# A hybrid decoder block on one core: x also loaded transposed, and the first norm's scale moved behind the projections

## The chip, the core and the metric

The kernel runs on one NeuronCore of a Trainium2 chip. Five engines work side by side, each through its own stream of instructions in order: TensorE (PE in the rows; its weight loads are PEld), VectorE (DVE), ScalarE (ACT), GpSimd (POOL) and SyncE (SP, which here only issues DMAs). They wait for one another by semaphores. The metric is the device time of one execution in microseconds (us); lower is better.

## The reference

One layer, 256 tokens, width 1024, float32. The part around the change:

```python
def rms_norm(x, w):
    y = xf * lax.rsqrt(jnp.mean(xf * xf, axis=-1, keepdims=True) + NORM_EPS)
    return (y * w.astype(jnp.float32)).astype(x.dtype)
...
proj = h @ w_in          # h = RMSNorm(x) of the layer, (256, 1024) @ (1024, 3336)
qa, ka, va, qb, kb, vb, qkv_c, z_c, b_c, a_c = jnp.split(proj, split_at, axis=-1)
```

Behind it come two small attentions (A: window of 128 with sinks, B: block-sparse, which at 256 tokens is causal), a gated DeltaNet with a causal convolution of width 4 on its queries, keys and values (`silu(conv(...))`) and a gate `silu(z_c)`, one output projection, a second norm, and a gated feed-forward network (up to 2 x 2816, convolution of width 3, gelu, down).

## The kernel before

Every weight comes from memory as float32 and is cut into two float32r parts, `hi` (a cast on ACT, line 129) and `lo` (the rest, a subtraction on DVE, line 130); so are the activations. A product is three passes: hi by hi, hi by lo, lo by hi. `load` takes a weight block of up to 2048 columns (1 MB) into one of three `raw` buffers (pool `wp`); the next load into that buffer waits on SP until the DVE has read the last of it.

The stages in the order of time:

1. Head (lines 207 to 291). x is loaded row-major as two tiles `xt[0]`, `xt[1]` of 128 tokens. For each tile: sums of squares (`square`, ACT and DVE), `rms_scale` (1/sqrt with one Newton step), the rows times that scale and the weight row `pw` (line 170), eight transposes on PE, then `h_evac` cuts the transposed result into `hT_hi` and `hT_lo` (lines 179, 180). `keep_warm` puts products of ones between. Then the first projection, `pb`: 48 products of 392 columns (line 287) from the weights `wb` (beta, a and the attentions' values).
2. Mixer (the words of `PLAN`). `gdn(c)` for 12 head parts: a projection `pg` (24 products of 256 columns, line 190), the convolution (`cv`: one ACT instruction, line 300, and three on DVE, line 302), a tanh (`th`, line 305), and line 306. `att(c)` for 7 pairs of attention heads: `pa`, brought out by ACT (lines 317, 319). `zgate(n)`: `pz`. Between them stand the small products of the DeltaNet; its inversion (`inv2`) goes round by `p_Y` on PE, `Y` on ACT (line 459), `p_D` on PE, `Dc` on DVE (line 465).
3. The output projection `pm`, the second norm and the feed-forward network (`pu`, `py`).

In the head and around the second norm the order on DVE, ACT and PE is the written one (`manual_schedule`). In the mixer a scheduler sets the order on each engine from its own estimate of durations, so that an edit there can change the order in many places. All DMAs are issued by SP in the written order.

Of the kernel before, what the change touches and what calls it, by code (L numbers as in the profile page):

```python
# [14 lines left out]
P = 128  # L15
# [28 lines left out]
WB0 = 1  # L44
WARM = [3, 2, 0]
# [6 lines left out]
def hybrid_block(ctx: ExitStack, tc, a):  # L52
# [40 lines left out]
    def rms_scale(pool, parts, name, meanwhile=None):  # L93
        """1 / sqrt(mean + eps): the square root's reciprocal, refined by a Newton step."""
# [70 lines left out]
    def norm_transpose(src, r, w, xn, n, name):  # L165
        """rows times r and w, transposed; the caller evacuates"""
# [35 lines left out]
    # =================== token mixer ===================  # L202
    with ExitStack() as mctx:
# [3 lines left out]
        pre = mp.tile([1, D], F32, tag="DL", name="pre")  # L207
        nc.sync.dma_start(pre, a["pre"])
        nc.sync.dma_start(xt[0], a["x"][0:P, :])
        nc.sync.dma_start(cst[:, 0:P], a["cst"][:, 0:P])  # L210
        nc.sync.dma_start(xt[1], a["x"][P:, :])
        nc.sync.dma_start(prm, a["prm"])
        ones = mp.tile([P, P], F32, name="ones")
        G.memset(ones, 1.0)
        def weights(src, c, total, per, store, name):
# [18 lines left out]
        raws = [load(a["wb"][:, c:c + 4].rearrange("p k c -> p (k c)"), f"wb{c}") for c in (0, 4)]  # L234
        nc.sync.dma_start(cst[:, P:], a["cst"][:, P:])
        nc.sync.dma_start(row, a["row"].to_broadcast([P, 12]))
        with tc.manual_schedule(engines={V.engine, A.engine, T.engine}):
            warm(cp, AF.Sqrt, zero, "warm_s")
            pw = []
            for j in range(2):  # L240
                pw.append(mm(f"n1_w{j}"))
                T.matmul(pw[j], ones[0:1, :], pre[0:1, j * 512:(j + 1) * 512], start=True, stop=True)
            xw = [mp.tile([P, D], F32, tag=("R", "gb")[n], name=f"n1_x{n}") for n in range(NT)]
            idle = mm("idle")

            def keep_warm(n):
                """products of ones that nobody reads: the array's clock slows down without work"""
                for i in range(n):
                    T.matmul(hs(idle, i % 4), ones, ones, start=True, stop=True)

            sq1 = [two(kp, "sq", f"n1_sq{n}") for n in range(NT)]

            def square(n):
                for j in range(2):
                    jk, x = kp.tile([P, 512], F32, tag="jk", name=f"n1_j{n}{j}"), xt[n][:, j * 512:(j + 1) * 512]
# [13 lines left out]
            h_evac(p0, 0, 0)
            h_evac(p0, 0, 1)  # L270
            half = 2 * W_BVA
            w = []
            if WB0:
                w = [split(raws[0], 0, half, "wb0", CH_M)]
            h_evac(p1, 1, 0)
            h_evac(p1, 1, 1)
            w += [split(raws[c // 4], c % 4 * W_BVA, half, f"wb{c}", CH_M) for c in (0, 2, 4, 6)[WB0:]]
            keep_warm(WARM[2])
# [31 lines left out]
        def att(c):  # L310
            """two heads' queries (scaled by -1/8 over their slope) or keys"""
# [23 lines left out]
        def gates():  # L335
# [6 lines left out]
            # softplus(y) = max(y, 0) + log1p(e), e = exp(-|y|); log1p(e) = 2 artanh(e / (2 + e))  # L342
# [27 lines left out]
        # decays, masked before the exponential; L = beta k k^T decay below the diagonal  # L370
        # (what L holds on and above the diagonal is never read)
# [15 lines left out]
        def keys():  # L387
            """token-major keys, their norms, L"""
# [190 lines left out]
        def zgate(n):  # L579
# [6 lines left out]
            A.activation(zt, pz, AF.Tanh, scale=0.5)  # L586
# [4 lines left out]
        def outs(n):  # L591
# [12 lines left out]
            f = newton(kp, fv, H, f"f{n}")  # L604
            for h in range(H):
# [121 lines left out]
    # =================== ConvGLU ===================  # L727
# [4 lines left out]
    def up_tokens(i, n):  # L732
        """a gate and up pair, token-major"""
# [166 lines left out]
def _pack(inp):  # L900
# [64 lines left out]
```

## Time and profile before

| what | us |
|---|---|
| median of 3 runs (351.55 to 355.4) | 351.56 |
| span of the profiled execution | 351.1 |
| PE busy in the span | 338.4 (96%) |
| DVE busy in the span | 257.0 (73%) |
| ACT busy in the span | 213.3 (61%) |

The span runs from the first to the last instruction of one profiled execution. The median of the runs is 0.46 us above it; times below are counted from the span's start. A row of the timeline is one instruction, or several alike in a row (x4), with start, length and, in brackets, how long its engine had been idle and what ended that.

### The profile page before, as it was taken

The numbers are of one execution on the slowest core, as the hardware profiler recorded it, in microseconds if no ns is written. First come the engines' busy times: TensorE is split into PE (matmuls) and PEld (weight loads), VectorE is DVE, ScalarE is ACT, GpSimd is POOL, SyncE is SP. The second block draws the span as 40 slices with busy tenths as digits, with TensorE's granted clock in tenths as the row PEclk, the third lists the DMA queues.
The fourth block names the chain that finished last, engine by engine and source line by source line (L and its number), as shares of the span: only waits on it lengthen the run. The fifth ranks groups of instructions, "written<-read, shape, count | busy, mean of one in ns | idle before, by whom it ended". The sixth has DMA issues, their size and how long they took to land.

```text
span 351.1 us, 7200 instructions
## 1 busy us (share of the span) xinstructions
PE 338.4 (96%) x2904; PEld 306.2 (87%) x2904; DVE 257.0 (73%) x531; ACT 213.3 (61%) x455; POOL 10.2 (3%) x26
## 2 busy tenths in 40 slices
PE   7899999999999999999999999999999999999992
PEld 4799898888788986779998999999999999999981
DVE  3969949987516767768879989887686866689443
ACT  4867588654656568755768777555464644655341
POOL 3030110000000000000000000000000000000000
PEclk9999999999999999999999999999999999999999
DMA  7797630073102736563153677772828363330002
GB/s 243 283 342 245 229 119 2 18 257 114 41 3 96 264 119 239 177 244 120 22 220 119 257 296 289 251 261 98 316 101 293 119 241 119 122 119 2 0 29 92
DMA packets 9107, 57.28 MB, mean 163 GB/s; under 512 B 1137, under 2 KB 1393, under 8 KB 2802
## 3 DMA queue, kind: packets, MB, share of 16 engines
q1 hardware_dynamic: 9074, 56.82, 45.2%
q8 instruction: 23, 0.38, 0.4%
q14 instruction: 10, 0.08, 0.1%
HBM read 55.77 MB, written 1.05 MB: 162 GB/s over the span
## 4 chain that ended last, share of the span: by engine, by line
PE 79%; ACT 8%; DVE 7%; DMA 4%; issue 2%; SPq 0%; DVEq 0%; ACTq 0%
PE pu L190 28%; PE py L693 16%; PE pm L693 6%; PE pg L190 4%; PE pa L190 4%; PE pz L198 3%; PE pt L739 3%; DMA wa_raw<-wa 2%; PE pb L287 2%; DVE u L770 2%; DMA xt<-x 2%; PE pv L663 1%; ACT pr L638 1%; PE p_D L463 1%; DVE wd_lo L130 1%
## 5 line engine op out<-in xcount | busy, mean ns | idle before, releaser
L190 PE MATMUL pu<-hT_hi,wu_hi 128*128 128x256 f32 x304 | 84.3, 277 | 0.0
L190 PE MATMUL pu<-hT_lo,wu_hi 128*128 128x256 f32 x304 | 84.1, 277 | 0.0
L190 PE MATMUL pu<-hT_hi,wu_lo 128*128 128x256 f32 x304 | 84.1, 277 | 0.0
L130 DVE TENSOR_TENSOR wu_lo<-wu_raw,wu_hi 128x1024 fp32r<-128x1024 f32 (+1 forms) x54 | 51.6, 984 | 19.2 <-ACT wu_hi L129 19.2
L190 PEld LDWEIGHTS pu<-hT_lo,wu_hi 128*128 128x128 f32 x304 | 57.2, 188 | 0.7
L190 PEld LDWEIGHTS pu<-hT_hi,wu_hi 128*128 128x128 f32 x304 | 57.1, 188 | 0.7
L190 PEld LDWEIGHTS pu<-hT_hi,wu_lo 128*128 128x128 f32 x304 | 57.1, 188 | 0.0
L129 ACT CAST wu_hi<-wu_raw 128x1024 fp32r<-128x1024 f32 (+1 forms) x54 | 44.6, 859 | 16.9 <-PE pu L190 15.3
L770 DVE SCALAR_TENSOR_TENSOR u<-pu,prm,u 128x255 f32<-128x255 f32 (+1 forms) x88 | 41.1, 478 | 5.8 <-ACT u L768 4.6
L693 PE MATMUL py<-wd_hi,mT_hi 128*128 128x512 f32 x88 | 34.4, 391 | 0.1
L693 PE MATMUL py<-wd_hi,mT_lo 128*128 128x512 f32 x88 | 34.5, 392 | 0.0
L693 PE MATMUL py<-wd_lo,mT_hi 128*128 128x512 f32 x88 | 34.3, 394 | 0.0
L130 DVE TENSOR_TENSOR wd_lo<-wd_raw,wd_hi 128x1024 fp32r<-128x1024 f32 (+1 forms) x28 | 27.2, 990 | 2.1 <-ACT wd_hi L129 2.1
L140 ACT CAST mT_hi<-ge 128x256 fp32r<-128x256 f32 x22 | 8.9, 406 | 32.0 <-DVE ge L774 32.0
L190 PE MATMUL pg<-hT_hi,wg_hi 128*128 128x256 f32 x96 | 27.6, 288 | 0.0
L190 PE MATMUL pg<-hT_hi,wg_lo 128*128 128x256 f32 x96 | 27.1, 282 | 0.0
L190 PE MATMUL pg<-hT_lo,wg_hi 128*128 128x256 f32 x96 | 26.9, 280 | 0.1
L768 ACT ACTIVATE u<-pu,prm 128x256 f32<-128x256 f32 x44 | 24.2, 559 | 3.8 <-PE pu L190 3.8
L129 ACT CAST wd_hi<-wd_raw 128x1024 fp32r<-128x1024 f32 (+1 forms) x28 | 22.7, 864 | 4.6 <-DMA wd_raw<-wd 4.6
L693 PEld LDWEIGHTS py<-wd_lo,mT_hi 128*128 128x128 f32 x88 | 16.5, 188 | 3.3
L693 PEld LDWEIGHTS py<-wd_hi,mT_hi 128*128 128x128 f32 x88 | 16.5, 188 | 3.3 <-ACT wd_hi L129 0.3
L693 PEld LDWEIGHTS py<-wd_hi,mT_lo 128*128 128x128 f32 x88 | 16.5, 188 | 3.1
(292 smaller groups left out, 708.3 us busy)
## 6 DMA issues: line engine op xcount, KB each, us to landing
wu_raw<-wu SPq DMA_DIRECT2D x22, 1024.0 KB, 4.9
wd_raw<-wd SPq DMA_DIRECT2D x11, 1024.0 KB, 4.9
wg_raw<-wg SPq DMA_DIRECT2D x6, 1024.0 KB, 5.8
wo_raw<-wo SPq DMA_DIRECT2D x4, 1024.0 KB, 5.0
wa_raw<-wa SPq DMA_DIRECT2D x3, 1024.0 KB, 7.5
wz_raw<-wz SPq DMA_DIRECT2D x2, 1024.0 KB, 5.0
wb_raw<-wb SPq DMA_DIRECT2D x2, 784.0 KB, 7.6
xt<-x SPq DMA_DIRECT2D x2, 512.0 KB, 4.4
```

The lines of the kernel that those rows point to most:

```text
L129: A.copy(hi[:, b:e], raw[:, c + b:c + e])
L130: V.tensor_tensor(lo[:, b:e], raw[:, c + b:c + e], hi[:, b:e].bitcast(F32), ALU.subtract)
L140: return A.copy(hi, src), V.tensor_tensor(lo, src, hi.bitcast(F32), ALU.subtract)
L190: T.matmul(pt[:, :S], x[:, k * P:(k + 1) * P], h[:, k, :], start=(i == 0), stop=(i == 3 * KT - 1))
L198: T.matmul(pt[:, :wd], h[:, k, n * P:(n + 1) * P], x[:, c:c + wd], start=(i == 0), stop=(i == 3 * KT - 1))
L287: T.matmul(pt[n][:, :W_BVA], h[:, k + b, n * P:(n + 1) * P], x[:, b * W_BVA:(b + 1) * W_BVA], start=(s == order[0] and b == 0), stop=(s == ...
L463: T.matmul(pD[sl, s * 32:s * 32 + 32], Y[sl, s, :], Dc[sl, s, :], start=True, stop=True)
L638: A.activation(pr[:, h, o0:o1], pr[:, h, o0:o1], AF.Exp, bias=nm[:, h, n:n + 1], scale=-1.0, accum_out=den[:, h, n:n + 1])
L693: T.matmul(acc[n][j], y[:, ms], x[:, c], start=(first and i == 0), stop=(last and i == 2))
L739: T.matmul(pt[:, :256], h[:, 4 * j + k, n * P:(n + 1) * P], x[:, k * 256:(k + 1) * 256], start=(j + s + k == 0), stop=(j + s + k == 6))
L768: A.activation(t, pu[c][:, :S], AF.Identity, scale=fw[:, c, 2:3], bias=fw[:, c, 3:4])
L770: V.scalar_tensor_tensor(t[:, s:], pu[c][:, :S - s], fw[:, c, 2 - s:3 - s], t[:, s:], ALU.mult, ALU.add)
```

## The change

x is brought in twice: as before in rows, and as `xT` with the 1024 features on the partitions. The host lays `xT` out. `hT_hi` and `hT_lo` are now cut straight from `xT` times the norm's weight (`pre`, now one column per feature, loaded by a DMA on ACT's queue), without the scale of a token; transposes, the row `pw` and `h_evac` fall away in the head. Squares and scale (`rx`) are worked out from the rows later, behind the cuts of `wb`. The scale is applied to products: to `ba` and `va` per token as they are brought out; by `rbc`, a tile that holds the scale along its columns on all partitions (built with a diagonal `dg` and two products `p_r`), to `pg` and `pa` on DVE; by `rh` and in `f` for the gate. `xT` and `wb` come in three pieces each, in turns, ahead of x.

```diff
+WARM = 8
+FIRST = ((0, 2), (2, 4), (4, 8))
+CH_B = W_BVA
...
-        pre = mp.tile([1, D], F32, tag="DL", name="pre")
-        nc.sync.dma_start(pre, a["pre"])
-        nc.sync.dma_start(xt[0], a["x"][0:P, :])
-        nc.sync.dma_start(cst[:, 0:P], a["cst"][:, 0:P])
-        nc.sync.dma_start(xt[1], a["x"][P:, :])
-        nc.sync.dma_start(prm, a["prm"])
+        pre = mp.tile([P, KT], F32, name="pre")
+        nc.scalar.dma_start(pre, a["pre"])
...
+        xT = mp.tile([P, KT, S], F32, tag="gb_xT", name="xT")
+        raws = [wp.tile([P, 2048], F32, tag="raw", name=f"wb{c}_raw") for c in (0, 4)]
+        for k0, k1 in FIRST:
+            nc.sync.dma_start(xT[:, k0:k1, :], a["xT"][:, k0:k1, :])
+            c = k0 % 4 * W_BVA
+            nc.sync.dma_start(raws[k0 // 4][:, c:c + (k1 - k0) * W_BVA], a["wb"][:, k0:k1].rearrange("p k c -> p (k c)"))
+        for n in range(NT):
+            nc.sync.dma_start(xt[n], a["x"][n * P:(n + 1) * P, :])
+        nc.sync.dma_start(cst[:, 0:P], a["cst"][:, 0:P])
+        nc.sync.dma_start(prm, a["prm"])
...
-            square(0)
-            r = rms_scale(kp, sq1[0], "n10", lambda: square(1))
-            keep_warm(WARM[0])
-            p0 = norm_transpose(xt[0], r, pw, xw[0], 0, "n1")
...
+            def h_split(k):
+
+                A.activation(hT_hi[:, k, :], xT[:, k, :], AF.Copy, scale=pre[:, k:k + 1])
+                V.scalar_tensor_tensor(hT_lo[:, k, :], xT[:, k, :], pre[:, k:k + 1], hT_hi[:, k, :].bitcast(F32),
+                                       ALU.mult, ALU.subtract)
+
+            half = 2 * W_BVA
+            w = []
+            for k in range(0, KT, 2):
+                h_split(k)
+                h_split(k + 1)
+                w.append(split(raws[k // 4], k % 4 * W_BVA, half, f"wb{k}", CH_B))
...
+            dg = kp.tile([P, NT, P], F32, tag="jk", name="dg")
+            for n in range(NT):
+                V.tensor_scalar(dg[:, n, :], ident, rx[:, n:n + 1], None, ALU.mult)
+            G.tensor_scalar(rh, rx, 0.5, None, ALU.mult)
...
+            pr = sm("p_r")
+            for n in range(NT):
+                T.matmul(hs(pr, n), ones, dg[:, n, :], start=True, stop=True)
             for n in range(NT):
-                V.tensor_copy(ba[:, n, :], pt[n][:, 384:392])
-                A.copy(va[:, n, :], pt[n][:, :384])
+                V.tensor_scalar(ba[:, n, :], pt[n][:, 384:392], rx[:, n:n + 1], None, ALU.mult)
+                A.activation(va[:, n, :], pt[n][:, :384], AF.Copy, scale=rx[:, n:n + 1])
+            A.copy(rbc, pr[:, :S])
...
+            m = kp.tile([P, S], F32, tag="cm", name=f"cm{c}")
+            V.tensor_tensor(m, pt[:, :S], rbc, ALU.mult)
             t = kp.tile([P, S], F32, tag="cv", name=f"cv{c}")
-            A.activation(t, pt[:, :S], AF.Copy, scale=cw[:, c, 3:4])
+            A.activation(t, m, AF.Copy, scale=cw[:, c, 3:4])
             for s in range(1, 4):
-                V.scalar_tensor_tensor(t[:, s:], pt[:, :S - s], cw[:, c, 3 - s:4 - s], t[:, s:],
+                V.scalar_tensor_tensor(t[:, s:], m[:, :S - s], cw[:, c, 3 - s:4 - s], t[:, s:],
                                        ALU.mult, ALU.add)
...
-                A.activation(aT[:, c, :], pt[:, :S], AF.Copy, scale=qsc[:, i:i + 1])
+                V.scalar_tensor_tensor(aT[:, c, :], pt[:, :S], qsc[:, i:i + 1], rbc, ALU.mult, ALU.mult)
             else:
-                A.copy(aT[:, c, :], pt[:, :S])
+                V.tensor_tensor(aT[:, c, :], pt[:, :S], rbc, ALU.mult)
```

The order on ACT in the head, from the last cuts of `wb` (`wb_hi`) to the first cuts of `wg`, the weights of `gdn`. Before:

```order
L129 CAST wb_hi_201<-wb_raw 128x784
L346 ACT_TABLE_LOAD
L346 ACTIVATE g_ea<-row 128x4
L129 CAST wg_hi_280<-wg_raw 128x1024
L129 CAST wg_hi_284<-wg_raw 128x1024
L129 CAST wg_hi_356<-wg_raw 128x1024
L291 COPY va<-pb_205 128x384
```

And now:

```order
L130 CAST wb_hi_164<-wb_raw 128x392 x2
L273 ACTIVATE n_j_172,sq_129<-xt_67 128x512
L273 ACTIVATE n_j_176,sq_129<-xt_68 128x512
L280 ACTIVATE rs<-rw 128x2
L361 ACT_TABLE_LOAD
L361 ACTIVATE g_ea<-row 128x4
L304 ACTIVATE va<-pb_190,rx 128x384
L304 ACTIVATE va<-pb_191,rx 128x384
L305 COPY rbc<-p_r 128x256
L355 ACTIVATE g_th<-ba 128x8
L130 CAST wg_hi_269<-wg_raw 128x1024
```

Three cuts of `wg` stood ahead of the first `va`; now all of them stand behind squares, scale, `va` and `rbc`.

The order on DVE from the scale of x to the first convolution, with the change; `cm` is the product times `rbc`:

```order
L284 SCALAR_TENSOR_TENSOR rx<-rs,rx 128x2
L287 TENSOR_SCALAR dg<-cst,rx 128x128 x2
L303 TENSOR_SCALAR ba<-pb_190,rx 128x8
L303 TENSOR_SCALAR ba<-pb_191,rx 128x8
L131 TENSOR_TENSOR wg_lo_270<-wg_raw,wg_hi_269 128x1024
L131 TENSOR_TENSOR wg_lo_274<-wg_raw,wg_hi_273 128x1024
L358 SCALAR_TENSOR_TENSOR g_ab<-g_y 128x8
L131 TENSOR_TENSOR wg_lo_350<-wg_raw,wg_hi_349 128x1024
L131 TENSOR_TENSOR wg_lo_354<-wg_raw,wg_hi_353 128x1024
L313 TENSOR_TENSOR cm_302<-pg_277,rbc 128x256
```

Before, the first two `wg_lo` stood ahead of `ba`; now all four stand behind the scale, and the first `cm` behind them.

The order on ACT in the mixer, around the inversion's `Y`. Before:

```order
L300 ACTIVATE cv_1131<-pg_1106,prm 128x256
L459 COPY Y_1174<-p_Y_1141 128x256
L305 ACTIVATE th_1103<-cv_1098 128x256
L129 CAST wz_hi_1525<-wz_raw 128x1024
L305 ACTIVATE th_1136<-cv_1131 128x256
L300 ACTIVATE cv_1248<-pg_1223,prm 128x256
L459 COPY Y_1291<-p_Y_1258 128x256
```

And now:

```order
L474 COPY Y_1183<-p_Y_1150 128x256
L315 ACTIVATE cv_1140<-cm_1138,prm 128x256
L320 ACTIVATE th_1110<-cv_1105 128x256
L320 ACTIVATE th_1145<-cv_1140 128x256
L130 CAST wz_hi_1538<-wz_raw 128x1024
L474 COPY Y_1302<-p_Y_1269 128x256
L315 ACTIVATE cv_1259<-cm_1257,prm 128x256
```

Each `Y` stood behind a `cv`; now it stands ahead of that `cv`.

## Rows read from the trace of the kernel before

**Rows 1.** The page: the span, and busy time of each engine.

```profile
span 351.1 us, 7200 instructions
...
PE 338.4 (96%) x2904; PEld 306.2 (87%) x2904; DVE 257.0 (73%) x531; ACT 213.3 (61%) x455; POOL 10.2 (3%) x26
```

**Rows 2.** Chain that ended last, its longest pieces up to 33 us: start, length, what.

```profile
2.00 5.44 DMA xt<-x
...
14.10 7.47 PE pb L287 x40
21.80 0.86 ACT va L291 x2
22.66 0.96 ACT wg_hi L129
23.66 1.23 DVE wg_lo L130
24.91 7.49 DMA wa_raw<-wa
```

**Rows 3.** Timeline of PE: the first of `pb`, the first of `pg`.

```profile
11.95 1.11 PE L287 MATMUL pb<-wb_hi,hT_hi 128*128 128x392 f32 x4
...
21.76 0.28 PE L190 MATMUL pg<-hT_hi,wg_hi 128*128 128x256 f32 x1
21.88 0.28 PE L190 MATMUL pg<-hT_lo,wg_hi 128*128 128x256 f32 x1
```

**Rows 4.** Groups of ACT by shape, up to 130 us: busy, mean ns of one.

```profile
L305 ACT ACTIVATE th<-cv 128x256 f32<-128x256 f32 x12 | 5.0, 419 | 3.0 <-DVE cv L302 2.7 <-DVE g_g L358 0.2
L129 ACT CAST wb_hi<-wb_raw 128x784 fp32r<-128x784 f32 x4 | 3.2, 856 | 0.0
```

**Rows 5.** Timeline of ACT in the head.

```profile
15.12 1.28 ACT L346 ACT_TABLE_LOAD   x1
...
16.53 1.98 ACT L129 CAST wg_hi<-wg_raw 128x1024 fp32r<-128x1024 f32 x2
```

**Rows 6.** Timeline of DVE in the head: squares, scale, and cuts of `wg`.

```profile
4.46 0.69 DVE L259 CUSTOM_DVE_ANT_0 n_j<-xt 128x512 f32<-128x512 f32 x1 [4.46 <-DMA xt<-x]
...
6.68 1.41 DVE L170 SCALAR_TENSOR_TENSOR n_x<-xt,n_r,n_w 128x512 f32<-128x512 f32 x2
...
17.60 2.36 DVE L130 TENSOR_TENSOR wg_lo<-wg_raw,wg_hi 128x1024 fp32r<-128x1024 f32 x2 [0.30 <-ACT wg_hi L129]
```

**Rows 7.** Stretches (start:end, length, busy time by engine, PEclk, DMA share, GB/s).

```profile
2.00:6.00 4.00, 3.56 (x4) 1.16 (x4) 1.12 (x5) 1.13 (x5) 0.94 (x2) 1.00 0.92 268
6.00:14.00 8.00, 6.98 (x33) 6.03 (x32) 6.85 (x17) 5.45 (x12) 0.99 (x3) 1.00 1.00 396
```

**Rows 8.** One stretch of a microsecond in the head, the same columns for DMA (PEclk, share, GB/s).

```profile
12.00:13.00 1.00, 1.00 1.10 446
```

**Rows 9.** Groups of DVE by shape, up to 130 us: busy, mean ns of one.

```profile
L302 DVE SCALAR_TENSOR_TENSOR cv<-pg,prm,cv 128x255 f32<-128x255 f32 x12 | 5.7, 476 | 0.3 <-ACT cv L300 0.3
...
L306 DVE SCALAR_TENSOR_TENSOR kT<-th,cv 128x256 f32<-128x256 f32 x4 | 1.7, 420 | 0.5 <-ACT th L305 0.5
...
L140 DVE TENSOR_TENSOR mT_lo<-pv,mT_hi 128x256 fp32r<-128x256 f32 x2 | 0.9, 426 | 3.0 <-ACT mT_hi L140 3.0
```

**Rows 10.** Stretches of the mixer (columns as in Rows 7).

```profile
21.80:60.00 38.20, 37.03 (x305) 35.49 (x304) 30.71 (x86) 28.06 (x77) 6.43 (x12) 1.00 0.51 174
60.00:75.00 15.00, 14.91 (x349) 13.11 (x349) 14.34 (x37) 9.91 (x30) 0.19 (x1) 1.00 0.29 89
```

**Rows 11.** Chain that ended last in the mixer, around two of the inversion's steps.

```profile
77.41 0.47 ACT cv L300
77.88 0.27 ACT Y L459
...
83.48 0.36 ACT cv L300
```

**Rows 12.** PE's last product, and its granted clock behind it (stretches).

```profile
344.22 0.40 PE L693 MATMUL py<-wd_lo,mT_hi 128*128 128x512 f32 x1
...
349.40:349.60 0.20, 0.00 (x0) 0.57 0.97 369
```

More of the change, by code (lines that the diff above doesn't have):

```diff
@@ L43 @@
 BORD = "00 01 02 10 11 12 20 21 22 30 31 32"
-WB0 = 1
-WARM = [3, 2, 0]
+WARM = 8
+FIRST = ((0, 2), (2, 4), (4, 8))
+CH_B = W_BVA
 WO = "40 41 50 51 60 00 10 20 30 70 u u 610 710 010 110 210 310 | 611 711 011 111 | 211 311"
@@ L233, in hybrid_block @@
         wz, wg, wa = [], [], []
-        raws = [load(a["wb"][:, c:c + 4].rearrange("p k c -> p (k c)"), f"wb{c}") for c in (0, 4)]
         nc.sync.dma_start(cst[:, P:], a["cst"][:, P:])
         nc.sync.dma_start(row, a["row"].to_broadcast([P, 12]))
+        rw = mp.tile([P, NT], F32, name="rw")
+        rx = mp.tile([P, NT], F32, name="rx")
+        rh = mp.tile([P, NT], F32, name="rh")
+        rbc = mp.tile([P, S], F32, name="rbc")
         with tc.manual_schedule(engines={V.engine, A.engine, T.engine}):
@@ L238, in hybrid_block @@
             warm(cp, AF.Sqrt, zero, "warm_s")
[L239 to L243, printed above, removed]
-            idle = mm("idle")
-            def keep_warm(n):
-                for i in range(n):
-                    T.matmul(hs(idle, i % 4), ones, ones, start=True, stop=True)
@@ L251, in hybrid_block @@
-            sq1 = [two(kp, "sq", f"n1_sq{n}") for n in range(NT)]
-            def square(n):
+            idle = mm("idle")
+            for i in range(WARM):
+                T.matmul(hs(idle, i % 4), ones, ones, start=True, stop=True)
+            sq1 = mp.tile([P, 2, NT], F32, name="sq1")
+            def h_split(k):
+                A.activation(hT_hi[:, k, :], xT[:, k, :], AF.Copy, scale=pre[:, k:k + 1])
+                V.scalar_tensor_tensor(hT_lo[:, k, :], xT[:, k, :], pre[:, k:k + 1], hT_hi[:, k, :].bitcast(F32),
+                                       ALU.mult, ALU.subtract)
@@ L254, in square @@
+            half = 2 * W_BVA
[5 more added lines that the diff above has]
+            for n in range(NT):
                 for j in range(2):
                     jk, x = kp.tile([P, 512], F32, tag="jk", name=f"n1_j{n}{j}"), xt[n][:, j * 512:(j + 1) * 512]
-                    if n or j:
-                        A.activation(jk, x, AF.Square, accum_out=sq1[n][j])
+                    if j:
+                        A.activation(jk, x, AF.Square, accum_out=sq1[:, j, n:n + 1])
@@ L258, in square @@
                     else:
                         V.tensor_tensor_reduce(out=jk, in0=x, in1=x, scale=1.0, scalar=0.0, op0=ALU.mult, op1=ALU.add,
-                                               accum_out=sq1[n][j])
-            square(0)
-            r = rms_scale(kp, sq1[0], "n10", lambda: square(1))
-            keep_warm(WARM[0])
-            p0 = norm_transpose(xt[0], r, pw, xw[0], 0, "n1")
-            keep_warm(WARM[1])
-            r = rms_scale(kp, sq1[1], "n11")
-            p1 = norm_transpose(xt[1], r, pw, xw[1], 1, "n1")
@@ L269, in hybrid_block @@
[L269 to L278, printed above, removed]
+                                               accum_out=sq1[:, j, n:n + 1])
+            V.tensor_scalar(rw, sq1[:, 0], -0.5 / D, -0.5 * EPS, ALU.mult, ALU.add)
@@ new lines, in hybrid_block @@
+            V.scalar_tensor_tensor(rw, sq1[:, 1], -0.5 / D, rw, ALU.mult, ALU.add)
+            rs = kp.tile([P, NT], F32, name="rs")
+            A.activation(rs, rw, AF.Sqrt, scale=-2.0)
+            V.reciprocal(rx, rs)
+            V.tensor_tensor(rs, rx, rx, ALU.mult)
+            V.tensor_tensor(rs, rs, rw, ALU.mult)
+            V.scalar_tensor_tensor(rx, rs, 1.5, rx, ALU.add, ALU.mult)
+            dg = kp.tile([P, NT, P], F32, tag="jk", name="dg")
+            for n in range(NT):
+                V.tensor_scalar(dg[:, n, :], ident, rx[:, n:n + 1], None, ALU.mult)
@@ L284, in hybrid_block @@
                 x, h = passes(*w[k // 2], hT_hi, hT_lo)[i]
-                for n in range(NT):
-                    for b in range(2):
+                for b in range(2):
+                    for n in range(NT):
                         T.matmul(pt[n][:, :W_BVA], h[:, k + b, n * P:(n + 1) * P], x[:, b * W_BVA:(b + 1) * W_BVA],
                                  start=(s == order[0] and b == 0), stop=(s == order[-1] and b == 1))
+            pr = sm("p_r")
             for n in range(NT):
-                V.tensor_copy(ba[:, n, :], pt[n][:, 384:392])
-                A.copy(va[:, n, :], pt[n][:, :384])
+                T.matmul(hs(pr, n), ones, dg[:, n, :], start=True, stop=True)
+            for n in range(NT):
+                V.tensor_scalar(ba[:, n, :], pt[n][:, 384:392], rx[:, n:n + 1], None, ALU.mult)
+                A.activation(va[:, n, :], pt[n][:, :384], AF.Copy, scale=rx[:, n:n + 1])
+            A.copy(rbc, pr[:, :S])
         def gdn(c):
@@ L585, in zgate @@
             zt = kp.tile([P, 512], F32, tag="jk", name=f"zt{n}")
-            A.activation(zt, pz, AF.Tanh, scale=0.5)
+            A.activation(zt, pz, AF.Tanh, scale=rh[:, n:n + 1])
             V.scalar_tensor_tensor(zg[:, n].rearrange("p h c -> p (h c)"), zt, 1.0, pz, ALU.add, ALU.mult)
@@ L604, in outs @@
             f = newton(kp, fv, H, f"f{n}")
+            V.tensor_scalar(f, f, rx[:, n:n + 1], None, ALU.mult)
             for h in range(H):
@@ L936, in _pack @@
     o["row"] = np.concatenate([g["swa_sinks"], g["dn_a_log"], g["dn_dt_bias"]], 1)
-    o["pre"] = g["mix_pre_norm"]
+    o["pre"] = np.ascontiguousarray(pp(g["mix_pre_norm"][0]))
     o["post"] = np.ascontiguousarray(np.stack([g["mix_post_norm"][0], g["ffn_pre_norm"][0]])[None])
@@ L940, in _pack @@
     o["x"] = np.ascontiguousarray(g["x"][0])
+    o["xT"] = np.ascontiguousarray(g["x"][0].reshape(S, KT, P).transpose(2, 1, 0))
     i, j = np.meshgrid(ar(P), ar(P), indexing="ij")
```

## The prediction

> **What bounds the kernel now.** I read the page first: PE is busy in 96% of a span of 351.1 us [rows 1], so a change pays only if PE's row of work starts sooner or has fewer holes. Then the chain that ended last, which shows where the start is set: x's second tile comes in for 5.44 us, norm and transposes follow, and from 14.10 on 40 products of `pb` run for 7.47 us, 0.187 us each [rows 2]. The timeline of PE gives the head's frame: `pb` begins at 11.95, the first `pg` at 21.76, and products of `pg` follow at 0.12 us, 24 to a head, 2.83 us [rows 3]. The 48 of `pb` need 9.0 us, so some 12.8 us of the first 21.76 hold nothing that counts. From 21.8 to 60 PE is idle 38.2 - 37.03 = 1.2 us, from 60 to 75 only 0.1 [rows 10]: behind the head PE runs nearly without holes, and what the head saves reaches the end of the run if the feeding of PE keeps up. The last thing to see is that the feeding is tight as well: the chain goes from `va` over a cut of `wg` to a DMA of 7.49 us [rows 2], because a raw buffer is loaded again only when DVE has read it, and DVE is busy 14.34 of 15 us from 60 to 75 [rows 10].
>
> **The change: the head.** Everything ahead of `pb` on PE goes: the products of `pw`, 16 transposes, their wait. What sets `pb` now is memory. The rows give 268 GB/s for the first 4 us of traffic and 396 after that [rows 7]. `xT` and `wb` together are 1.05 + 1.61 = 2.65 MB; with 1.07 MB by 6 us the rest takes 1.58/0.396 = 4.0 us, to 10.0, and x's two tiles were used 0.5 and 1.3 us after their last byte by the same count (at 4.46 [rows 6] and 7.44 [rows 2]); with 0.9, the last piece of `wb` is there at L = 10.9. Its earlier pieces are cut while later ones arrive. Behind L, ACT casts two pieces of 392 columns, two of `hT_hi` and two more of `wb`. A cast of 784 takes 0.86 and one instruction of 256 columns 0.42 [rows 4], so 0.43 and 0.37 at back-to-back pace, 2.5 us in all; DVE ends its last cut at L + 3.2. PE needs 24 products, 4.5 us, from L + 0.5 on, so `pb` ends at L + 5 = 15.9, some 5.9 us sooner than before.
>
> But `pg` can't follow. ACT and DVE take in order: squares, 0.61 each on DVE, to L + 4.4; then the scale. From the start of the square to the scaled rows took 6.68 - 4.46 = 2.2 us with one square in it [rows 6], so 1.6 for the scale, to L + 6.0; `dg`, two small instructions, to L + 6.5; `p_r` on PE to L + 7.0. On ACT a table load of 1.28 [rows 5] runs beside that, then come `g_ea`, `va` (0.86 [rows 2]), `rbc` (0.37), `g_th`: L + 7.9. Only now is `wg` cut: `wg_hi` 1.0 us (1.98 for two [rows 5]), `wg_lo` 1.18 (2.36 for two [rows 6]). Four products of `pg` need `hi` alone, the fifth waits for `wg_lo`, at L + 10.1. From there PE runs on, with 4 x 0.12 us done: as if it had begun at L + 9.6 = 20.5. Before it was 21.76. **The head gains 1.2 us.** Cover: `wg`'s own first load stands behind 5.44 MB now, 1.05 more than before; 6 + (5.44 - 1.07)/0.396 + 0.9 = 17.9, against 18.8 (L + 7.9) at which ACT wants it. So two chains end within a microsecond of each other, and taking one away would give little. With 396 GB/s from 2 us on L would be 1.3 us earlier; with 268 up to 10 us, 1.3 later: the head gains between 2.5 and -0.1 us.
>
> The Trainium skill ("DMA: Bandwidth & Descriptors", section "Bandwidth") holds that loads from memory are bound by about 358 GB/s per core, not by the 435 of the fabric. The rows here show 446 in a microsecond of the head [rows 8], so it is not taken; with 358 from 6 us on, L would be an estimated 0.4 us later and the head's gain 0.8.
>
> **The change: DVE and ACT in the mixer.** Each of 12 heads gets a `cm` on DVE: 256 columns from a product and a second operand, 0.43 as the nearest row has it, while its three `cv` now read a copy in SBUF: 0.42 instead of 0.476 each [rows 9]. Net 12 x (0.43 - 0.16) = 3.2 us. Seven `aT` move from ACT to DVE, 0.43 each: 3.0 us. DVE has 6.2 us more work in the mixer, ACT 3 us less. Bounds for PE: nothing, if all of it falls into DVE's holes, or 6.2 us. Up to 60 us DVE has 38.2 - 30.71 = 7.5 us of holes and about half of the new work; from 60 to 75 it has 0.66 [rows 10] and gets four `cm` less 12 savings, 1.1 us. I take 0.7 us: the second stretch's overhang of 0.4 and a little for waits at `cm`, with DVE standing still until `pg` is done.
>
> Against it stands a thing the order shows: each `Y` of the inversion now precedes the `cv` that it stood behind. On the chain those two `cv` are worth 0.47 and 0.36 us [rows 11]: -0.8. ACT is strictly in order, so this holds unless the new `cv`, which waits for `cm`, holds up a later `Y`; then it is 0. A raw buffer of `wg` comes free some 2 us later than before, but its load then has 5.7 us of PE's work on the other pair as cover. The new factor in `f` (two instructions on 128x4) I take at nothing: PE has `pa` products meanwhile; uncovered it is 0.3 us. The feed-forward part is untouched.
>
> **Sum:** -1.2 - 0.8 + 0.7 = -1.3 us. The span of 351.1 becomes 349.8; the median lies 0.46 above that execution's span, so 351.56 - 1.3 = 350.3 us. By the bounds (head -2.5 to +0.1, inversion -0.8 to 0, DVE 0 to 1.8, above which it is the first rival) it is 348.3 to 353.5.
>
> **Rivals.** *DVE becomes the bound* (ends slower). Place: 33 to 90 us, where `cm` sits in front of everything that uses a product. If the whole 6.2 us falls on PE: 351.56 - 1.2 + 6.2 = 356.6; half of it gives 353.5. It decides when DVE's holes between 60 and 75, 0.66 us, don't take what is added there and PE stands waiting for a `lo`. For it: 14.34 of 15; against it: products are released by one `cm` instead of four readers, and the holes ahead of 60.
>
> *Memory is faster than the rows of the ramp.* The slow start [rows 7] may come from the small pieces of `cst` and `prm`, which now stand behind x. With 446 GB/s throughout [rows 8] from 1.6 us on, L = 8.5, `wg` lands at 14.7, and PE is as if it began at 18.1: -3.7, with the inversion -0.8 and nothing for DVE: 347.1 us. Not more, as the row of squares, scale, `va` and cuts stays. For it: no small piece is ahead of `wb`. Against it: pieces are smaller than x's rows were.
>
> *The clock of PE falls.* Between the end of `pb` and `wg_lo`, 15.9 to 21.0, PE has only `p_r` and four products. Behind the last product of the run, at 344.62, the granted clock was half, 1.2 instead of 2.4 GHz, from about 349.4 on [rows 12]; all of the head ran at 1.00 [rows 7]. If it falls here, 24 to 48 products of `pg` take 0.24 instead of 0.12 us: +2.8 to +5.7, so about 353.1 to 356. The hole is 5 us long but not empty. The Trainium skill ("TensorE: Matmul & The Clock Gate", section "HAM oscillation — how this bites in real kernels") says that waits for DMA between bursts of products put the clock down and make the next burst start slow; here, by it, the sum would be the same 353.1, and the trace of before, whose head had holes too, does not show it.
>
> **How the numbers follow.** Forecast 350.3 (348.3 to 353.5): 0.55. Faster memory, 347.1: 0.17. DVE as the bound, 353.5 to 356.6: 0.17. Clock: 0.08. Something else: 0.03. The range takes in the second case and the lower half of the third and fourth: 346.6 to 354.4. Two per cent, 7.0 us, is about what a measurement of this kernel can tell from no change. A gain beyond 344.5 would need the whole 5.9 us of `pb` and more: 0.02. A loss beyond 358.6 needs all of DVE's work and a slow clock on PE's path: 0.04. Within: 0.94.
>
> **What would show it.** `pb` starting near 6 and ending near 16 us; a hole on PE from there to about 20 to 21, ended by DVE's `wg_lo` and not by a DMA; the first continuous `pg` a microsecond before 21.76. In the mixer `Y` without a `cv` ahead of it, and no new waits of PE on DVE over half a microsecond. It is wrong if `wg_hi` waits for its DMA for over a microsecond, if the granted clock leaves 1.00 before 30 us, or if DVE has no hole from 33 to 75 and PE gets one.

## The result, and the profile after

The changed kernel takes 354.67 us (median of 20 runs, 353.29 to 359.02) against 351.75 for the kernel before beside it (20 runs, 351.3 to 355.7). The ratio is 1.0061, 95% interval 1.0035 to 1.0086: slower by about 0.6%, where 1.3 us less was forecast, and 0.3 us outside the stated range. The ratios in this text are taken from the fast runs alone and are no quotients of the medians (here 1.008); two runs of the changed kernel, 358.94 and 359.02 us, are slow ones. The profiled execution took 355.75, a microsecond over the median, with a span of 354.0 us.

The page of the changed kernel, the lines that answer to [rows 1]: the span is 2.9 us more while PE's busy time is 1.2 less, although the head's old work on PE is gone: some of what is left must have become longer, and there are 4.1 us more of holes.

```profile
span 354.0 us, 7204 instructions
...
PE 337.2 (95%) x2894; PEld 307.6 (87%) x2894; DVE 262.4 (74%) x556; ACT 214.8 (61%) x454; POOL 10.3 (3%) x27
```

PE's timeline in the changed kernel (start, length, line, operation, in brackets the idle time ahead of it and who ended it), the lines that answer to [rows 3]. `pb` begins at 6.33 and ends at 17.1 (said: near 6 and 15.9). Then comes the hole, with `p_r` alone in it. The first `pg` starts at 21.22, half a microsecond sooner than before; but products follow each other at 0.21 us until 27.6, and at 0.12, the pace before, only from there.

```profile
6.33 1.68 PE L297 MATMUL pb<-wb_hi,hT_hi 128*128 128x392 f32 x4 [1.53 <-ACT wb_hi L130]
7.80 1.51 PE L297 MATMUL pb<-wb_hi,hT_lo 128*128 128x392 f32 x4
...
16.20 0.88 PE L297 MATMUL pb<-wb_lo,hT_hi 128*128 128x392 f32 x4
18.41 0.77 PE L301 MATMUL p_r<-dg,ones 128*128 128x128 f32 x4 [1.33 <-DVE dg L287]
21.22 0.58 PE L191 MATMUL pg<-hT_hi,wg_hi 128*128 128x256 f32 x1 [2.04 <-ACT wg_hi L130]
...
22.76 0.41 PE L191 MATMUL pg<-hT_hi,wg_lo 128*128 128x256 f32 x1
22.97 0.41 PE L191 MATMUL pg<-hT_hi,wg_hi 128*128 128x256 f32 x1
...
29.71 0.28 PE L191 MATMUL pg<-hT_hi,wg_hi 128*128 128x256 f32 x1
29.82 0.28 PE L191 MATMUL pg<-hT_lo,wg_hi 128*128 128x256 f32 x1
```

Stretches of a microsecond of the same kernel; the third number from the end is the granted clock of PE. It falls at about 20.8, after a stretch in which PE has next to nothing, to 0.50 (1.2 of 2.4 GHz), and is back at about 27.6. In the kernel before this column is 1.00 up to 349 us.

```profile
19.00:20.00 1.00, 0.18 (x2) 0.00 (x0) 0.00 (x0) 1.00 (x3) 0.19 (x1) 1.00 1.07 442
20.00:21.00 1.00, 0.00 (x0) 0.00 (x0) 0.00 (x0) 1.00 (x3) 0.39 (x2) 0.88 0.98 410
21.00:22.00 1.00, 0.78 (x2) 0.50 (x2) 0.80 (x1) 1.00 (x3) 0.00 (x0) 0.50 0.85 352
...
27.00:28.00 1.00, 1.00 (x8) 1.00 (x7) 0.31 (x1) 0.00 (x0) 0.00 (x0) 0.71 0.99 393
28.00:29.00 1.00, 1.00 (x11) 1.00 (x10) 1.00 (x3) 0.85 (x2) 0.69 (x1) 1.00 1.01 410
```

Every run is on record with the mean of its granted clock. It is 0.981 to 0.993 in the 20 runs of the changed kernel, and 0.994 to 0.998 in 79 of the 80 runs of the kernel before that stand beside the experiments (0.990 in one). So the other runs of the changed kernel had more of the low clock too. The mean takes in every fall, that behind the last product as well, so it does not say where a run's clock fell.

What the hole waits for is seen on ACT and DVE of the same kernel (answers to [rows 5, 6]). The last piece of `wb` is there at 11.81, and from it the row goes over casts, squares, `rs`, table load, `va` and `rbc` to the cut of `wg` at 20.11; DVE is done with the first `wg_lo` at 22.4.

```profile
11.81 0.94 ACT L130 CAST wb_hi<-wb_raw 128x392 fp32r<-128x392 f32 x2 [1.04 <-DMA wb_raw<-wb]
...
17.24 1.28 ACT L361 ACT_TABLE_LOAD   x1
...
18.80 1.05 ACT L304 ACTIVATE va<-pb,rx 128x384 f32<-128x384 f32 x2
19.75 0.37 ACT L305 COPY rbc<-p_r 128x256 f32<-128x256 f32 x1
...
20.11 3.90 ACT L130 CAST wg_hi<-wg_raw 128x1024 fp32r<-128x1024 f32 x4
```

```profile
21.20 2.36 DVE L131 TENSOR_TENSOR wg_lo<-wg_raw,wg_hi 128x1024 fp32r<-128x1024 f32 x2 [2.29 <-ACT wg_hi L130]
```

Groups of DVE by shape up to 130 us in the changed kernel (busy, mean ns of one), which answer to [rows 9]: the `cv` cost as much from SBUF as they did from the product's bank, so `cm` comes on top in full, 5.0 us.

```profile
L317 DVE SCALAR_TENSOR_TENSOR cv<-cm,prm,cv 128x255 f32<-128x255 f32 x12 | 5.7, 475 | 0.3 <-ACT cv L315 0.3
...
L313 DVE TENSOR_TENSOR cm<-pg,rbc 128x256 f32<-128x256 f32 x12 | 5.0, 418 | 2.4 <-PE pg L191 2.3
```

Where the time came from, by the first product of each kind on PE in the two profiled executions (before, after): `pg` 21.8, 21.2; `pa` 33.1, 35.5; `p_D` of the inversion 64.5, 66.0; `pz` 87.9, 90.8; `pt` 160.0, 162.6; last `py` 344.2, 346.8. So 2.4 us are lost between `pg` and the first `pa`, and about as much is still missing at the end. In most runs here the time lies 1.8 us above the execution's span; by that (an estimate) the profile of the kernel before, with its 351.1, shows an execution some 1.3 us longer than the median one, and its marks are late by up to as much. In the inversion there is one thing more, PE's waits from 60 to 92 us (in all, how often, the longest): two stops inside `p_D` for which the trace names nothing that PE waited for (0.7 in one stop in the kernel before).

```profile
PE p_D L478 <- issue: 2.1, 2, 1.1
PE p_D L478 <- ACT Y L474: 0.7, 1, 0.7
```

### The profile page after: what moved, and what is told of

It reads as the page before. It is cut to its first block, busy times and chain, and to the rows that moved or that the text cites. A ratio compares the mean times of both kernels' runs of the same rounds, so it can differ in the third digit from the quotient of the medians.

```text
span 354.0 us, 7204 instructions
## 1 busy us (share of the span) xinstructions
PE 337.2 (95%) x2894; PEld 307.6 (87%) x2894; DVE 262.4 (74%) x556; ACT 214.8 (61%) x454; POOL 10.3 (3%) x27
## 4 chain that ended last, share of the span: by engine, by line
PE 77%; DVE 10%; ACT 7%; DMA 2%; issue 1%; SPq 1%; DVEq 0%; POOL 0%; ACTq 0%
PE pu L191 28%; PE py L709 16%; PE pg L191 6%; PE pm L709 6%; PE pa L191 3%; PE pt L755 3%; PE pz L199 3%; DMA wb_raw<-wb 2%; DVE u L786 2%; PE pv L679 1%; DVE cv L317 1%; DVE wg_lo L131 1%; PE p_D L478 1%; ACT wg_hi L130 1%; DVE wd_lo L131 1%
## 5 line engine op out<-in xcount | busy, mean ns | idle before, releaser
L191 PE MATMUL pg<-hT_hi,wg_hi 128*128 128x256 f32 x96 | 29.0, 303 | 2.2 <-ACT wg_hi L130 2.2
L191 PE MATMUL pg<-hT_lo,wg_hi 128*128 128x256 f32 x96 | 28.0, 292 | 0.0
L191 PEld LDWEIGHTS pg<-hT_hi,wg_hi 128*128 128x128 f32 x96 | 19.3, 201 | 3.2 <-ACT wg_hi L130 2.7
L709 PEld LDWEIGHTS py<-wd_hi,mT_hi 128*128 128x128 f32 x88 | 16.5, 188 | 3.5 <-ACT wd_hi L130 0.5
L709 PEld LDWEIGHTS py<-wd_lo,mT_hi 128*128 128x128 f32 x88 | 16.5, 188 | 3.3
```

Source lines behind the costliest of these rows:

```text
L191: T.matmul(pt[:, :S], x[:, k * P:(k + 1) * P], h[:, k, :], start=(i == 0), stop=(i == 3 * KT - 1))
L709: T.matmul(acc[n][j], y[:, ms], x[:, c], start=(first and i == 0), stop=(last and i == 2))
```

## The experiments

Theory A: the hole lets PE's clock fall, and `pg` at half speed is the loss. Theory B: DVE's added work in the mixer is the loss. Two more came up on the way, C (the order that the scheduler gives the mixer) and D (idle products help by something other than filling the hole). "The kernel before" is the one run beside each group, 351.84 to 352.07.

**Idle products in the hole.**

```diff
+            for i in range(6):
+                T.matmul(hs(idle, i % 4), ones, ones, start=True, stop=True)
             pr = sm("p_r")
             for n in range(NT):
                 T.matmul(hs(pr, n), ones, dg[:, n, :], start=True, stop=True)
+            for i in range(11):
+                T.matmul(hs(idle, i % 4), ones, ones, start=True, stop=True)
```

> The changed kernel with 17 idle products of `ones` in the hole of PE's row: 6 between `pb` and `p_r`, 11 between `p_r` and `pg`. They compute nothing that is used. Theory A (PE's clock falls because of the hole between the end of `pb`, 17.0, and the start of `pg`, 21.2, and that is the loss): the granted clock stays at 1.00 from 20 to 28 us, the first `pa` product starts at about 33.0 instead of 35.5, and the time comes to 351.3 to 352.3, 2.4 to 3.4 under the changed kernel. Theory B (the added work of DVE in the mixer, 12 `cm` and 7 `aT`, is the loss): the first `pa` may come earlier, but the gain is gone by the end of the mixer, and the time stays at 353.8 to 354.9.

Measured: 351.48 us, ratio 0.9982 (0.9957 to 1.0007). In the profiled execution the clock is 1.00 from 12 to 340 us (in the head, ahead of the hole, it is 0.50 from 7.6 to 11.0), `pg` starts at 20.7 and the first `pa` at 32.2. The time is 3.2 us under the changed kernel by the medians, 2.8 by the ratios, as theory A has it. Theory B is out as the main cause, since DVE's work is all there. But the order of the mixer is another one here, which leaves theory C.

**The cut of `wg` ahead of `va`, without and with idle products.**

```diff
             G.tensor_scalar(rh, rx, 0.5, None, ALU.mult)
+            weights(a["wg"], 0, N_GDN, 2, wg, "wg0")
```

> The changed kernel with the first cut of `wg` ahead of `va`, `rbc` and `ba` in the rows of ACT and DVE; nothing is added. Theory A: the cut starts when ACT has loaded its table, about 17.3 to 18.5, instead of at 20.1, so `pg` can start at 18.5 to 19.5, the hole is half as long, and either the clock does not fall (then pg starts 2 us sooner at full clock, first `pa` at 31.5 to 32, time 349.5 to 350.5) or it falls for a shorter stretch (352 to 353.5). Theory B: `pg` starts sooner, but the `cm` and `cv` of DVE and ACT wait for `rbc` and run later; the time is 353.5 to 355.

> Both edits: the cut of `wg` ahead of `va`, and idle products in what is left of the hole (6 ahead of `p_r`, 4 behind it). Theory A: the clock stays at 1.00, `pg` starts at about 19.5, the first `pa` at about 31.3; time 349 to 350.5, 4 to 5.5 under the changed kernel and 1 to 2.5 under the kernel before. Theory B: no lower than 353.

Measured: 353.66 (352.08 to 355.05) without, ratio 1.0046 (1.0016 to 1.0076); 349.36 with 6 and 4 idle products, ratio 0.9938 (0.9921 to 0.9954), and 350.37 when it was run again, twelve times (0.9949, 0.9911 to 0.9988).

> The kernel with the first cut of `wg` ahead of `va` and 10 idle products, once more in more rounds, as a version to keep: Theory A gives what it gave, 349 to 350.5, a ratio to the kernel before of 0.992 to 0.997.

Without idle products `pg` starts at 19.1, two microseconds sooner, and in the profiled run (352.25) the clock holds from 11.1 us to the end of the work; still the time is 352 to 355, above what theory A gave for that case; the median is what theory B said. But the same edit with the hole filled, and with all of DVE's work, is 3 to 4 us faster, as theory A had it and theory B excluded. So an earlier start alone is not what pays, though by the traces the mixer's order differs between these two as well. Whether the clock fell behind the hole in the runs that took 354 is not shown: only one was profiled, and the mean clock (0.986 to 0.990 in the four runs from 353.66 on, 0.993, 0.993 and 0.988 in the three below 352.5) takes in the falls in the head and behind the last product.

**The scale left out.** The first kernel, with `m = pt` in `gdn` and `aT` copied by ACT.

> The first of these kernels (17 idle products in the hole) with the scale of the tokens left out behind `pg` and `pa`: `cv` reads the product's bank and `aT` is copied by ACT, as in the kernel before, so the 12 `cm` and 7 `aT` leave DVE (about 8 us of its work). What is left out is the factor of the norm on those rows. Theory A: the added work lies beside PE's, so this comes to within 0.7 of the kernel with the scale, at 351 to 352. Theory B: it is 2 or more faster than that one.

Measured: 352.99, ratio 1.0037 (1.0019 to 1.0055): 1.5 us *slower* than with the scale. Neither theory had that. PE's waits from 30 to 60 us in this kernel name a new one, for the gates' `DL` on ACT; in the kernel with the scale none of them is over half a microsecond.

```profile
PE p_G L425 <- ACT DL L397: 2.1, 2, 1.1
```

The instructions of the mixer stand in another order here, because the scheduler plans with what there is; so a kernel with less work for DVE is not simply a faster one. That made theory C a question of its own.

**The hole filled by 9 and by 10.** One row of the first edit, with 9 ahead of `p_r` and none behind it, then with 10. The run with 9 was meant to fill the hole and leave the order as it is in the changed kernel.

> The changed kernel with 9 idle products between `pb` and `p_r` and none behind `p_r`. Every other instruction stands in the order of the changed kernel, on each engine (in the first of these runs, with 17, the scheduler also put the mixer's `cm`, `cv` and cuts in another order). The products fill 17.0 to 19.2, and the hole that is left is 19.6 to 21.2. Theory A (the clock alone): the clock stays at 1.00, the first `pa` comes at 32.3 to 32.8 in place of 35.5, all later marks are 2.4 to 3.2 earlier, and the time is 351.6 to 352.4. Theory C (the gain of the kernel with 17 came from its order): the time stays at 353.8 to 354.9. Theory B (DVE's added work): the same, 353.8 to 354.9.

> One idle product more, 10. With it the scheduler gives the mixer the order of the kernel with 17 idle products. Theory A: the clock stays as in the run with 9, and what differs from it is the order's part: 0 to 1.0 faster, 351.2 to 352.2. Theory C: 2 to 3 faster than the run with 9, at 351 to 352, while that stays above 353.8.

Measured: 351.57 with 9, ratio 1.0002 (0.9976 to 1.0029); 351.90 with 10, 0.9990 (0.9949 to 1.0031). The whole gain is there with both. But the order did not stay. By the traces the kernels with 9, 10 and 17 idle products run every engine's instructions in one and the same order, and it is not that of the changed kernel. ACT shows it, first in the changed kernel, then in that with 9: a cut of `wa` stands ahead of the first `cv` in the one, and both cuts stand behind it in the other.

```profile
24.45 1.04 ACT L130 CAST wa_hi<-wa_raw 128x1024 fp32r<-128x1024 f32 x1 [0.34 <-DMA wa_raw<-wa]
...
28.15 0.51 ACT L315 ACTIVATE cv<-cm,prm 128x256 f32<-128x256 f32 x1 [2.65 <-DVE cm L313]
```

```profile
25.48 0.51 ACT L317 ACTIVATE cv<-cm,prm 128x256 f32<-128x256 f32 x1 [1.71 <-DVE cm L315]
25.90 1.98 ACT L130 CAST wa_hi<-wa_raw 128x1024 fp32r<-128x1024 f32 x2
```

So what the two texts above say of the order with 9 is not what ran: all three kernels with the hole filled have the other order, and they do not tell theory A from theory C. Within one order the clock can still be seen. Of the ten runs with 9, the five with a mean granted clock of 0.997 or 0.998 have a median of 351.12 us, the five with 0.992 or 0.993 one of 352.49. With 10 it is 351.86 (0.997 and 0.998) against 352.68 (0.989 and 0.990). With 17 no such difference is to be seen: 0.989 goes with 351.44 to 351.78, 0.994 to 0.996 with 351.12 to 351.93.

PE's timeline and two stretches of the kernel with 9 (each idle product and each `p_r` stands as two instructions): PE is at work to 19.4, the hole that is left is 1.5 us, and in this execution the clock stays. The first `pa` comes at 33.1, where 32.3 to 32.8 was expected.

```profile
16.75 2.17 PE L300 MATMUL idle<-ones 128*128 128x128 f32 x18
18.75 0.61 PE L303 MATMUL p_r<-dg,ones 128*128 128x128 f32 x4
20.87 0.38 PE L191 MATMUL pg<-hT_hi,wg_hi 128*128 128x256 f32 x1 [1.50 <-ACT wg_hi L130]
```

```profile
20.00:21.00 1.00, 0.13 (x1) 0.13 (x2) 0.15 (x1) 1.00 (x2) 0.35 (x2) 1.00 0.98 410
...
22.00:23.00 1.00, 1.00 (x9) 0.99 (x9) 1.00 (x2) 1.00 (x2) 0.00 (x0) 1.00 0.32 115
```

**Nine at the start, and four in the hole.** In the first `WARM = 8` becomes 17; the second has `range(4)` where the kernel above has 9. By their traces both do keep the order of the changed kernel.

> A control for the run with 9 idle products in the hole: the changed kernel with 9 more idle products at the start instead (17 in place of 8, ahead of `pb`, from about 3.8 to 6.0), none in the hole. The order of all other instructions is that of the changed kernel. Theory A: the hole between `pb` and `pg` is as before, the clock falls in it as it did, and the time stays at 354 to 355.2. If idle products help by anything else than filling the hole (theory D: they keep PE warm in the first microseconds, or move PE's row), it comes down to 351.5 to 352.5 as with 9 in the hole.

> 4 idle products in place of 9 ahead of `p_r`, in the same order of instructions. They end at about 18.0, before `p_r` at 18.4 to 19.0, so PE's last work ahead of the hole ends at the same time as in the changed kernel, and only the first part of the hole is filled. Theory A as it stands (an almost empty stretch is what lets the clock fall) does not say where the line lies: if the clock holds, 351.3 to 352.3; if it falls later or for a shorter time, 352.5 to 354.5. A time between, with runs of both kinds, would say that the hole is then near the line.

Measured: 355.22 with nine at the start, ratio 1.0053 (1.0015 to 1.0091), the changed kernel's time. So nine products ahead of `pb` do not help, and theory D falls in that form; that nine in the hole help by the order that goes with them is theory C. With four in the hole 353.90 (351.98 at best), ratio 1.0019 (0.9980 to 1.0059), between the two. Stretches, first of the kernel with nine at the start, then of that with four in the hole: in the first the clock falls at 20.7, in the second only at 22.1, and stays low for 3.4 us.

```profile
20.00:21.00 1.00, 0.51 (x2) 0.30 (x2) 0.77 (x1) 1.00 (x2) 0.00 (x0) 0.84 1.00 418
```

```profile
21.00:22.00 1.00, 0.61 (x4) 0.60 (x5) 1.00 (x2) 1.00 (x2) 0.00 (x0) 1.00 0.67 279
22.00:23.00 1.00, 1.00 (x7) 1.00 (x6) 1.00 (x3) 1.00 (x2) 0.06 (x1) 0.57 0.12 33
...
25.00:26.00 1.00, 1.00 (x8) 1.00 (x8) 0.13 (x1) 0.00 (x0) 0.23 (x1) 0.72 0.99 401
```

Note the stretch from 22 to 23: PE is fully at work when the clock falls there. The fall comes behind the hole, not in it. One of the ten runs with four has a mean clock of 0.996, as high as the kernel before, and takes 351.98; the other nine have 0.986 to 0.993, and none of them takes less than 353.14. This kernel has the order of the changed one, so here the loss goes with the clock while the order stays. But it is one run, and it was not profiled.

**The mixer's half alone.** The kernel before with `rbc` as a tile of ones and the `cm` and `aT` of the changed kernel.

> The kernel before with the mixer's half of the change alone: `rbc` is a tile of ones, and the 12 `cm` and 7 `aT` are on DVE as in the changed kernel; its head is as it was, and the result is the same. Theory A: DVE's extra work (some 6 us) lies beside PE's, so the time stays within 0.7 of the kernel before: 351.1 to 352.5. Theory B: it is slower by 2 or more, 353.8 or later. Theory C would show as up to 1.5 either way, since the scheduler gives this kernel an order of its own.

Measured: 353.32, ratio 1.0048 (1.0007 to 1.0089): 1.5 us slower than the kernel before, between what the two theories said. PE has no new wait on `cm` over half a microsecond; its longest in the mixer is 1.2 us for `Y`. So the added work, with the order that goes with it, is not free. But its price and that of the kernel without the scale (1.2 us over the kernel before, with the new head) don't add up to the changed kernel with its hole filled, which stands at 0.0: each of these kernels has an order of its own, and no run here shows what an order is worth by itself.

**The hole filled with PE's own next work.** The first load of `wg` goes ahead of x's rows, its cuts and 48 products ahead of the scale.

```diff
+        wg0 = load(a["wg"][:, 0:2].rearrange("p t c -> p (t c)"), "wg0")
         for n in range(NT):
             nc.sync.dma_start(xt[n], a["x"][n * P:(n + 1) * P, :])
...
+            for c in range(2):
+                wg.append(split(wg0, c * 1024, 1024, f"wg{c}", CH_M))
...
+            pg = [mm(f"pg{c}") for c in range(2)]
+            for c in range(2):
+                proj_cm(pg[c], wg[c])
             pr = sm("p_r")
```

> The changed kernel, with the first load of `wg` ahead of the loads of x in rows, and its two cuts and the first 48 products of `pg` ahead of the squares, `p_r`, `va` and `rbc`: no idle products, but the hole is filled with PE's own next work. Theory A: `pg` starts at 17.5 to 18.5, right behind `pb`; the clock stays at 1.00; the first `pa` comes at 29 to 30.5 and the time is 347 to 349, if the scale that comes later (`rbc` at 23 to 24.5) does not hold `cm` up; with that, 349 to 351. Theory B: no better than 352, since DVE's work is the same and begins later.

Measured: 356.74, ratio 1.0123 (1.0056 to 1.0190), the slowest of all (4 runs, 347 to 351 expected). `pg` does start at 16.2. But the hole has moved. PE's timeline: behind `p_r` it has two products until the third and fourth heads' weights are cut, at 25.0, and these cuts stand on ACT behind `va` and `rbc`, on DVE behind `cm`.

```profile
21.63 0.61 PE L307 MATMUL p_r<-dg,ones 128*128 128x128 f32 x4
23.75 0.39 PE L191 MATMUL pg<-hT_hi,wg_hi 128*128 128x256 f32 x1 [1.50 <-ACT wg_hi L130]
...
25.00 0.39 PE L191 MATMUL pg<-hT_hi,wg_lo 128*128 128x256 f32 x1 [0.76 <-DVE wg_lo L131]
```

```profile
24.00:26.00 2.00, 1.24 (x8) 1.04 (x8) 2.00 (x4) 2.00 (x4) 0.00 (x0) 0.86 0.26 102
26.00:28.00 2.00, 2.00 (x11) 2.00 (x11) 2.00 (x5) 2.00 (x5) 0.00 (x0) 0.50 0.00 0
```

The clock falls again, and once more at 83.5 us, behind a stop of 3.1 us in `p_D` of the unnamed kind:

```profile
82.01 0.28 PE L485 MATMUL p_D<-Dc,Y 32*32 32x32 f32 x9 [3.06 <-issue]
```

The moved hole is not what makes this kernel the slowest. Its first `p_D` comes at 63.0, level with the kernels with 9 and 17 idle products (63.1 and 62.6); from there to the first `pz` it takes 26.8 us, against 21.7 and 22.5. The loss lies in the inversion, where the stop and the second fall are. So my expectation of the time was wrong, but this run does not show that own work is worse than idle products.

**A version to keep.** The kernel with the cut of `wg` ahead of `va` and 6 and 4 idle products, and `wg`'s first load ahead of the rest of the constants on SP:

```diff
-        nc.sync.dma_start(cst[:, P:], a["cst"][:, P:])
-        nc.sync.dma_start(row, a["row"].to_broadcast([P, 12]))
...
             weights(a["wg"], 0, N_GDN, 2, wg, "wg0")
+            nc.sync.dma_start(cst[:, P:], a["cst"][:, P:])
+            nc.sync.dma_start(row, a["row"].to_broadcast([P, 12]))
```

> The same with the first load of `wg` ahead of the loads of the rest of the constants (482 KB, some 1.2 us at 400 GB/s) and of `row` on SP; ACT's table load then stands behind the first cut, since its `g_ea` waits for `row`. Theory A: `pg` starts at 18.0 to 19.0 in place of 19.4, the clock stays, and the time is 348.3 to 349.5, unless the mixer's order, which the scheduler makes anew, takes 0.5 to 1 back.

Measured: 349.85 (349.38 to 352.38, 12 runs), ratio 0.9918 (0.9884 to 0.9952). It beats both kernels, the one before by 0.8% and the changed one by some 1.4%. It is a little over the 348.3 to 349.5 expected, and the intervals do not tell it from the kernel without this last edit (0.9911 to 0.9988). The cut of `wg` begins at 16.42, ahead of the table load, and in the profiled execution the clock holds from 11 us on; `pg` starts at 19.2, since the idle products now end later than the cut asks for.

## Why the prediction was wrong

**The step that failed** is the clock of PE, which the sum put at nothing: it took the products of `pg` behind the hole at 0.12 us, and left the clock to the third rival at a chance of 0.08. In the profiled execution the clock is at 0.50 from 20.8 to 27.6, and 23 products at 0.213 in place of 0.118 us make 2.2 us on PE's row, which from 22.8 on has no hole in which to hide them. The rival had the place and the mechanism right. Its price, 2.8 to 5.7, was too high, and that the time lies in its 353.1 to 356 is in part luck, as the -1.3 of the rest was not there either (below).

How much of the loss is the clock's is shown less well. With the hole filled the time is 351.57, and with the same nine products put elsewhere it is 355.22; between the changed kernel and the filled hole lie 3.1 us by the medians, 2.1 by the ratios. The products account for 2.2 of that. But filling the hole also gave the mixer another order, so these runs by themselves don't part the clock from the order. For the clock speak the lengths of the products, the first `pa` behind them, 2.4 us later than in the kernel with 9, and the one run of 351.98 in the changed kernel's order.

Two arguments held the chance down. "The hole is not empty": `p_r` and four products didn't keep the clock up. "All of the head ran at 1.00 [rows 7]": the column said so, but it was no evidence. In the changed kernel four products of `pb` take 1.51 us at 7.80 and 0.88 at 16.20, and in the kernel before PE's timeline has eight equal transposes at 1.91 and at 1.44 us (these begin behind a wait), all with the column at 1.00:

```profile
7.55 1.91 PE L173 MATMUL n_p<-cst,n_x 128*128 128x128 f32 x8
...
10.76 1.44 PE L173 MATMUL n_p<-cst,n_x 128*128 128x128 f32 x8 [0.44 <-DVE n_x L170]
```

In the kernel with 17 idle products four products of `pb` take the same 1.51 us, and there the column does show 0.50:

```profile
8.10 1.51 PE L297 MATMUL pb<-wb_lo,hT_hi 128*128 128x392 f32 x4
```

```profile
8.00:9.00 1.00, 1.00 (x4) 1.00 (x4) 0.76 (x3) 0.84 (x2) 0.00 (x0) 0.50 1.06 439
```

So PE had been slow in both heads for some microseconds, and the column did not say so. The Trainium skill ("TensorE: Matmul & The Clock Gate", section "HAM oscillation — how this bites in real kernels") was cited for this rival and set aside; the trace agrees with it, with 0.50 from 21 to 27 us, though the wait here was for ACT and not for a DMA. The same page (section "Seeing it yourself") warns that clock events in a trace can't always be trusted; the 1.51 us under a column of 1.00 agree with that too.

**The head.** `pb` from 6.3 to 17.1 (said: 6 to 15.9), the hole up to the cut of `wg` by ACT and DVE and by no DMA: as said. L was 11.81 in the profiled execution and 10.76 to 11.40 in the ten other kernels with these loads, around the 10.9 of the sum. From L to the first `wg_lo` done it took 10.6 us, said 10.1. By the prediction's own measure `pg` runs as if begun at 21.9, where 20.5 was said and 21.76 had been before. So the -1.2 is nothing in this execution; in the kernel with 17 idle products, with L at 11.1, the first `wg_lo` is done at 21.5, which makes it -0.7.

**DVE in the mixer.** The step that `cv` reads SBUF at 0.42 was wrong (475 ns), so DVE got 5.0 + 3.2 = 8.2 us more, not 6.2. Its price, with an order of its own, measured +1.5 by the medians (0.2 to 3.1 by the ratio), against +0.7 taken and bounds of 0 to 1.8. PE got no wait on `cm`, and 0.4 us on `aT`. From 60 to 75 us DVE is busy 14.55 of 15, 0.2 more than before [rows 10], so the stretch was full already; PE's holes there grew from 0.1 to 0.75, the waits for `Y` among them, and not the 3 to 6 us of the first rival.

```profile
60.00:75.00 15.00, 14.25 (x342) 12.33 (x342) 14.55 (x46) 10.33 (x36) 0.00 (x0) 1.00 0.22 73
```

**The inversion.** The -0.8 is not to be seen: PE's waits from 55 to 92 us name `Y` with 0.7 us in the changed kernel and 0.7 in that with 9 idle products, and not at all in the kernel before. The two `cv` ahead of `Y` on the chain [rows 11] were no time that PE had waited.

**The sum without the clock** said -1.3. Measured it is 0.0 (-0.8 to +1.0) with 9 idle products, and -0.6 (-1.5 to +0.2) with 17. Both kernels have the other order. In it, apart from the clock, the change is worth nothing that can be told from zero.

**What stays open.** No kernel was run that fills the hole in the changed kernel's order, so theory C is not excluded. The stops inside `p_D` were 1.7 to 2.2 us in the three profiled runs with the changed kernel's hole open or in part, and 0.3, 0.5 and 0.9 with 9, 10 and 17 idle products, so they are perhaps 1.5 us of the profiled 355.75. The first three are also the three in the changed kernel's order, so the stops may go with the order. What makes them isn't named in any trace, and no run took them apart. What the mixer's two halves cost each by itself could not be had free of the order that goes with them.

## What to carry to other kernels

When a change takes work from the head of a busy engine and puts a chain of other engines there, look first at what TensorE does meanwhile: a few microseconds that are nearly empty can cost as much at half clock as the head gave. Fill such a hole with products that nobody reads, and test it by two controls, the same products elsewhere and the same order of everything else, and read from the trace that the order is the same; here it was not. Real work brought forward only moves the hole if what comes behind it isn't ready. And read the clock from the length of like products, not from its column alone.

## What the runs showed of the hardware

The clock did not fall at a fixed time after TensorE's row thinned out: 5.0 us after the last dense row with four idle products in the hole (17.1 to 22.1), 3.7 in the changed kernel (17.1 to 20.8), 4.2 with nine at the start (16.5 to 20.7). It stayed low for 6.8 us in the changed kernel and 3.4 in the other two, though products were dense in all three from about 22 on. The `cv` instructions on 128 x 255 elements cost DVE the same from SBUF (475 ns) as from a product's bank (476). And the scheduler's order for the whole mixer turned over on a few idle products more in the head: with 4 it is that of the changed kernel, with 9, 10 and 17 another.
